# Six edits to the instruction order of a one-core hybrid encoder layer: two loads, one scaling pass, one transpose pair, three splits, four merges and five casts

## The chip, the cores and the metric

The kernel runs on one core of a Trainium2 chip. The metric is the device time of one execution in microseconds (us), as the median of several runs. The engines are named as in the profile: PE (TensorE, matmuls), DVE (VectorE), ACT (ScalarE), POOL (GpSimd) and SP (SyncE, whose queue issues nearly all DMAs here).

## The reference

One layer of a bidirectional hybrid encoder, for 1024 tokens of width 1024:

```python
x = layer_norm(x, emb_ln_g, emb_ln_b)
proj = x @ w_in                                  # 1024 -> 5120
q, k, v, z_a, u, z_b, g_a, g_b = split(proj)     # 4x512, 2x512, 2x1024
attn = neighbourhood_attention(q, k, v, rpb)     # 8 heads x 64, window 8 x 16 on a 16 x 64 grid
y_a  = attn * silu(z_a)
u    = centred_depthwise_conv(u, conv_w, conv_b)
h    = rg_lru(u, ..., forward) + rg_lru(u, ..., reverse)   # gates, then a linear scan over the tokens
y_b  = h * silu(z_b)
m    = sigmoid(g_a + b_merge[0]) * (y_a @ w_ba) + sigmoid(g_b + b_merge[1]) * (y_b @ w_bb)
out  = layer_norm(ALPHA * x + m @ w_out, ln_g, ln_b)
```

## The kernel before

All is in fp32 accuracy: each operand of a product is split into a high and a low part (a rounding copy, called a cast, and a subtraction, called a low split), and each product is three matmuls (`mm3`, line 139): high x high, high x low, low x high. The instruction order of every engine is the order in which the program records it; no scheduler moves anything. So a line that is written earlier stands earlier in its engine's queue, and every engine, SP too, works through its queue in order.

The stages, with their place in the profiled span:

- Prologue (to about 80 us): LayerNorm statistics of the token tiles, turning them, and the products for v, q and k. Tiles 4 to 7 are loaded already turned; their mean and scale are brought into rows by two transposes of a broadcast column (`spread(i)`, line 322, into the bank bcp) and a copy (`spread_copy`, line 326). The scale `ln6e` comes from a chain of small DVE operations that ends in line 245.
- The remaining columns of `x @ w_in`, in 17 pairs of 7 products (a Strassen-like scheme, so that a 2 x 2 block product takes 7 products): 119 slots plus 4, each 12 matmuls of 512 columns on PE. `pair` p uses weights `wa_*`, `ws_*` (tags a11, s2, s3, s1, a12, s4, a22) that are loaded, summed on DVE (`s_sum`), cast on ACT or POOL (`s_hi`, line 476) and split on DVE or POOL (`s_lo`, line 133). `evacuate` takes finished products off their banks: the copies `u` on ACT, the sums `c` and `s` on DVE (lines 775, 811). `c` frees the bank that the next pair of products writes.
- Beside the slots, at slots that tables name, run other steps (`todo`): the conv, gates and scans of the RG-LRU (lines 842 to 937; POOL's pass in line 918 stands behind a memset on DVE in line 917), and the token passes: `tokens_in` loads tile hw4 to hw7, `tokens_scaled` is ACT's pass over 128x1024 (line 1046), `tokens_gained` POOL's four (line 1050), `tokens_out` the store. `TOKENS_AT` holds, for each tile, the slots of the load, the scaling and the four gains.
- Slots 116 and on load q, k and the bias of the first heads (`load_k`, `load_head`: qs, ks, bias). At the end of the pairs (`ending(k)`) the first two products of the lru branch are made into the banks mb100 and mb101; `b_gate` (line 1137) multiplies them with the merge gate `g` on DVE: m <- g, mb. `g` was stored to DRAM (gb_d) as slots made it and is loaded by `g_load` (line 1124).
- Attention, 8 heads of 8 units. A unit has the scores on PE (line 1214), softmax on DVE and ACT, transposes of the probabilities (line 1236) and the values (`acc`, line 1262), in two value banks. `finish_a` (line 1273) reads a finished value bank into `attn` on DVE. Between them PE gets the remaining products of the lru branch as a filler; their `b_gate` waits in the list `pending` for the next unit's place for it, as `finish_a` and its followers wait in `todo`.
- Then the products of the attention branch, the merge, w_out, and the last LayerNorm (from about 530 us).

The lines that the change touches in the loop over slots and in the loop over units are these:

```python
        for o in lows:          # slots: the low split of the slot before
            s_lo(*o)
        lows = [prep]
...
        for f in pending:       # units: b_gate, and the split of the next weights
            f()
        pending.clear()
        for f in todo.pop(unit, ()):   # finish_a, finish_v, gated
            f()
```

Of the kernel before, what the change touches and what calls it, by code (L numbers as in the profile page):

```python
# [33 lines left out]
GATE_AT = (21, 31, 42, 52, 63, 73, 84, 94)  # L34
LATE_AT = (109, 109, 110, 111, 112)
HEAD_AT = 116
TOKENS_AT = ((1, 3, (4, 4, 5, 5)), (2, 5, (6, 6, 7, 7)), (3, 7, (8, 8, 9, 9)), (9, 11, (12, 12, 13, 13)))
RATES_AT = 14
LO_POOL = ("a11", "a22")
HI_POOL = ("a12", "s2", "s1", "s3", "s4")  # L40
FIRST_POOL = ("a22", "s4")
FIRST_ACT = (1, 2, 3)
U_PAIRS = (1, 6)
BLOCKS = (1, 0, 6, 4, 3, 2, 5, 7)
SCORES = (0, 1, 2, 5, 6, 7, 3, 4)
# [26 lines left out]
def encoder_kernel(ctx, tc, x, xt, gb1, gb, w_qk, w_v, w_s, w_ba, w_bb, w_gate, smalls, bias, w_out, out):  # L72
# [245 lines left out]
    def spread(i):  # L318

        bcp[i] = pst.tile([P, HALF], F32, tag="bank", name=f"bcp{i}")  # L320
        for z, col in enumerate((sts[i][1][:, 0:1], sts[i][2])):
            PE.transpose(bcp[i][:, z * P:(z + 1) * P], col.to_broadcast([P, P]), ident[:])
# [12 lines left out]
    def affine(i, *kks):  # L335
        for kk in kks or BOTH:
            tps[i, kk] = pst.tile([P, HALF], F32, tag="bank", name=f"tp{i}_{kk}")
            for k4 in range(4):
                k = 4 * kk + k4
                g, b = (sm[:, SM_LN + 8 * z + k:SM_LN + 8 * z + k + 1] for z in range(2))  # L340
                A.activation(tps[i, kk][:, k4 * P:(k4 + 1) * P], xts[i][:, k, :], AF.Identity, bias=b, scale=g)
            turn_hi(i, kk)
            if kk == 0:
                tag = ("a22", "a21", "a12", "a22")[i - 4]
                tt[i, 3] = wsp.tile([P, 4, P], F32, tag=tag, bufs=2 if tag == "a22" else 1, name=f"t3_{i}")[:]
                A.copy(tt[i, 3], tp4(i, 0))
# [30 lines left out]
    def f(t, i):  # L377
        return t[:, :, ti(i)].bitcast(F32)
# [27 lines left out]
    def v_part(i, kind, ks):  # L406

        if i not in vos:
            vos[i], vn[i] = bank(f"v{i}"), 0
        for k in ks:  # L410
            a = blocks[k // 4][i // 4][kind == "a"][:, k % 4, ti(i)]
            PE.matmul(vos[i][:], a, wv[kind == "w"][k][:], start=vn[i] == 0, stop=vn[i] == 23)  # L412
            vn[i] += 1
# [37 lines left out]
    s_a, s_w = {}, {}  # L451
# [21 lines left out]
    def s_hi(p, o):  # L473
        if p < N_PAIR:
            s_w[p, o] = pair(wsp, [P, 4, P], f"w{o}_{p}", tag="w" + o)
            (G.tensor_copy if p and o in HI_POOL and p not in FIRST_ACT else A.copy)(s_w[p, o][0][:], s_a[p, o])

    def s_lo(p, o):
        if p < N_PAIR:
            hi, lo = s_w[p, o]  # L480
            lo_of(G if o in (LO_POOL if p else FIRST_POOL) else V, lo[:], s_a[p, o], hi[:])
# [149 lines left out]
    v_hi(2)  # L631
    v_part(3, "w", K1)
    v_part(3, "a", K0)
    spread(6)
    spread_copy(6)
    affine(4, 0)
    ln_sums(7)
    centred(6)
    v_lo(2)
    v_store(2)  # L640
    affine(4, 1)
    sts_rest(7)
    v_part(3, "a", K1)
    v_hi(3)
    lows_t(4)
    v_lo(3)
# [178 lines left out]
    todo = {}  # L825

    def at(slot, pos, f):
        todo.setdefault((slot, pos), []).append(f)
# [147 lines left out]
    def yb_lo(t):  # L976
        hi, lo = late["yb"]
        lo_of(V, lo[:, t, :], lo[:, t, :].bitcast(F32), hi[:, t, :])
# [92 lines left out]
    for t, slot in enumerate(LATE_AT[1:]):  # L1071
        at(slot, 1, lambda t=t: yb_load(t))
        at(slot + 2, 1, lambda t=t: yb_hi(t))
        at(slot + 3, 0, lambda t=t: yb_lo(t))
    at(HEAD_AT, 1, head_pool)
    at(HEAD_AT, 1, lambda: load_k(0))
    at(HEAD_AT, 1, lambda: load_head(1))
# [43 lines left out]
    def g_load(which, j, n, **kw):  # L1121
        if j < NK:
            g = mt[which, j, n] = ev.tile([P, HALF], F32, name=f"g{which}{j}{n}", **(kw or dict(tag="z", bufs=5)))
            SP.dma_start(g[:], (ga_d, gb_d)[which][j][:, n * HALF:(n + 1) * HALF])
# [16 lines left out]
    def ending(k):  # L1141

        if k == 0:
            for pl in (hts.pop(), hts.pop(), wsp, hb):
                pl.release()
            late["mp"] = pool("mp")
        if k == 2:
            b_load(1, 2)
            for n in range(2):
                g_load(1, 1, n)  # L1150
        if k < 2:
            g_load(1, 0, k)
            late["o", k] = bank(f"mb10{k}")
            run(b_group(1, 0, k, late["yb"], late["o", k]))
        if 0 < k < 3:
            b_gate(1, 0, k - 1, late["o", k - 1])
# [3 lines left out]
    for slot in range(7 * N_PAIR + 4):  # L1160
        p, k = divmod(slot, 7)
        if k == 0 and p < N_PAIR:
            takers[p], ub[p] = takes[p](), {}
        done = (p, k - 1) if k else (p - 1, 6)
        prep = (p + 1, OPS[k - 1]) if k else (p if p else N_PAIR, OPS[6])
        rest = evacuate(*done) if slot <= 7 * N_PAIR else []
        s_hi(*prep)
        for f in todo.pop((slot, 0), ()):
            f()
        for f in squashes:  # L1170
            f()
        squashes = rest[:1]
        stores[slot + 2] = rest[1:]
        if p < N_PAIR:
            product(p, k)
        for o in lows:
            s_lo(*o)
        lows = [prep]
        for f in stores.pop(slot, ()):
            f()  # L1180
        if k < 4:
            s_sum(p + 1, ("s1", "s2", "s3", "s4")[k])
        elif k == 4:
            s_load(p + 2, "a11", "a21", "a12", "a22")
        for f in todo.pop((slot, 1), ()):
            f()
        if p == N_PAIR:
            ending(k)
# [38 lines left out]
    def exped(h, t):  # L1227
        w = P * len(near(t))
        A.activation(probs[h % 2][t][:], scs.pop((h, t))[:, :w], AF.Exp, bias=sums[h][0][:, t:t + 1], scale=-1.0,  # L1229
                     accum_out=sums[h][1][:, t:t + 1])  # L1230
# [112 lines left out]
    for unit in range(-NT, H * NT + PV_LAG):  # L1343
        h, c = divmod(unit, NT)
        before, b = divmod(unit - 1, NT)
        pv, pb = divmod(unit - PV_LAG, NT)

        if -1 <= before < H - 1:
            biased(before + 1, SCORES[b])
        if 0 <= before < H:  # L1350
            turned_lo(before, BLOCKS[b])
        if 0 <= h < H:
            turned(h, BLOCKS[c])
            if c == 3:
                sums_turned(h, tps[h, BLOCKS[c]])
        if 0 <= pv < H:
            values(pv, BLOCKS[pb])
            if pb in (5, 7) and pv < H - 1:
                for d, f in enumerate((finish_a, finish_v) + ((gated,) if pv % 2 else ())):
                    todo.setdefault(unit + d + 1, []).append(lambda f=f, pv=pv, g=pb // 7: f(pv, g))  # L1360
            elif pb in (5, 7):
                for d, f in enumerate(last_half(pb // 7)):
                    todo.setdefault(unit + d + 1, []).append(f)
        if 0 <= h < H:
            turned_hi(h, BLOCKS[c])
            if c == 2:
                sums_inverted(h)
            elif c == 3:
                sums_out(h)
        if -1 <= before < H - 1:  # L1370
            exped(before + 1, SCORES[b])
        for f in pending:
            f()
        pending.clear()
        for f in todo.pop(unit, ()):
            f()
        if -1 <= h < H - 1:
            score(h + 1, SCORES[c])
        if 0 <= h < H:
            if c == (4 if h == H - 1 else 5 if h % 2 else 7):  # L1380
                sums_in(h)
            elif c == (6 if h == H - 1 else 7) and h % 2:
                for n in range(2):
                    gate(h // 2, n)
        if c == 0 and 0 <= h:
            load_head(h + 2)
            if h % 2:
                load_za(h // 2)
        if c == PV_LAG and 0 <= h and h % 2 == 0:
            load_v(h // 2 + 1)  # L1390
        want = sum(FILL[:h + 1]) + FILL[min(h + 1, H)] * (c + 1) // NT
        while filled < want and next(fill, True) is None:
            filled += 1
        if unit == H * NT:

            for pl in (late["hd"], late["hd0"], late["ybp"]):
                pl.release()
            wop = pool("wop", "right")
            raw = {}

            def w_load(o, c):
                k, n = ("b11", "b12", "b21", "b22").index(o) // 2 * 4 + c, int(o[2]) - 1
                t = raw[o, c] = wop.tile([P, HALF], F32, tag=f"{o}{c}", name=f"w{o}_{c}")
                SP.dma_start(t[:], w_out[k * P:(k + 1) * P, halves[n]])

            b_load(0, 1)
            for n in range(2):
                g_load(0, 0, n, **(dict(tag="u3", bufs=1) if n else {}))
            for c in range(2):
                w_load("b12", c)  # L1410
                w_load("b11", c)
# [468 lines left out]
```

## Time and profile before

| what | value |
|---|---|
| runs | 660.69 us median of 3 (659.84 to 660.7) |
| profiled execution | 660.51 us; its span 658.6 us |
| granted PE clock | 0.997 |
| busy, share of the span | PE 98%, DVE 81%, ACT 62%, POOL 62% |
| DMA | 118.66 MB, mean 180 GB/s |

The span runs from the first to the last instruction on the core; the execution's time has 1.9 us more. Busy time of a pipelined engine counts overlapping instructions once. In rows of the timeline, the first number is the start in us of the span, the second the duration, and a bracket says how long the engine was idle before and what ended it. Numbers such as L1137 are lines of the kernel before.

### The profile page before, as it was taken

The numbers are of one execution on the slowest core, as the hardware profiler recorded it, in microseconds if no ns is written. First come the engines' busy times: TensorE is split into PE (matmuls) and PEld (weight loads), VectorE is DVE, ScalarE is ACT, GpSimd is POOL, SyncE is SP. The second block draws the span as 40 slices with busy tenths as digits, with TensorE's granted clock in tenths as the row PEclk, the third lists the DMA queues.
The fourth block names the chain that finished last, engine by engine and source line by source line (L and its number), as shares of the span: only waits on it lengthen the run. The fifth ranks groups of instructions, "written<-read, shape, count | busy, mean of one in ns | idle before, by whom it ended". The sixth has DMA issues, their size and how long they took to land.

```text
span 658.6 us, 9484 instructions
## 1 busy us (share of the span) xinstructions
PE 646.0 (98%) x3089; PEld 539.3 (82%) x3089; DVE 536.8 (81%) x850; ACT 409.4 (62%) x731; POOL 409.5 (62%) x331
## 2 busy tenths in 40 slices
PE   8999999999999999999999999999999999999994
PEld 6888878888888887888788888789888888888884
DVE  7989998995998699879988696277887876994777
ACT  5578655467786676778566834277777744574243
POOL 6569669824676476567656555012652549989956
PEclk9999999999999999999999999999999999999998
DMA  8765577333344124531461547897976288333023
GB/s 325 289 220 162 190 245 260 119 127 112 127 144 135 42 98 124 180 117 59 159 209 61 196 159 269 309 341 261 365 278 239 65 305 295 117 116 127 17 111 128
DMA packets 54064, 118.66 MB, mean 180 GB/s; under 512 B 5680, under 2 KB 10368, under 8 KB 52480
## 3 DMA queue, kind: packets, MB, share of 16 engines
q1 hardware_dynamic: 53696, 117.67, 51.5%
q8 instruction: 24, 0.39, 0.2%
q10 hardware_dynamic: 320, 0.40, 0.2%
q14 instruction: 24, 0.20, 0.1%
HBM read 82.36 MB, written 35.68 MB: 179 GB/s over the span
## 4 chain that ended last, share of the span: by engine, by line
PE 89%; DVE 8%; DMA 2%; issue 1%; ACT 0%; SPq 0%; DVEq 0%; ACTq 0%
PE a L139 32%; PE mb L139 12%; PE s L139 12%; PE v L412 6%; PE x L139 5%; PE w L139 5%; PE acc L1262 4%; PE q L139 3%; PE s L1214 3%; PE pt L1236 3%; PE g L884 2%; DMA g<-gb_d 1%; DVE ws_l L133 1%; DVE uc L842 1%; PE tp L358 1%
## 5 line engine op out<-in xcount | busy, mean ns | idle before, releaser
L139 PE MATMUL a<-ht_h,ws_h 128*128 128x512 f32 x136 | 53.1, 390 | 0.0
L139 PE MATMUL a<-ht_l,ws_h 128*128 128x512 f32 x136 | 52.9, 389 | 0.0
L139 PE MATMUL a<-ht_h,ws_l 128*128 128x512 f32 x136 | 52.9, 389 | 0.0
L139 PE MATMUL a<-b_h,wa_h 128*128 128x512 f32 x136 | 52.9, 389 | 0.0
L139 PE MATMUL a<-b_h,wa_l 128*128 128x512 f32 x136 | 52.9, 389 | 0.0
L139 PE MATMUL a<-b_l,wa_h 128*128 128x512 f32 x136 | 52.9, 389 | 0.0
L1224 DVE CUSTOM_DVE_ANT_0 sc<-s,bias 128x384 f32<-128x384 f32 (+1 forms) x64 | 33.4, 523 | 20.3 <-PE s L1214 11.4
L1243 ACT CAST pt_h<-pt 128x384 fp32r<-128x384 f32 x64 | 29.0, 454 | 23.8 <-PE pt L1236 19.3
L1229 ACT ACTIVATE p<-sc,summ 128x384 f32<-128x384 f32 (+1 forms) x64 | 37.8, 591 | 6.2 <-DVE summ L1224 5.9
L139 PE MATMUL mb<-ya,wb_h 128*128 128x512 f32 x128 | 39.5, 389 | 0.0
L992 POOL CAST wb_h<-wb 128x512 fp32r<-128x512 f32 x9 | 7.0, 780 | 49.5 <-DMA wb<-in_w_bb_dram 49.5
L133 DVE TENSOR_TENSOR pt_l<-pt,pt_h 128x384 fp32r<-128x384 f32 x64 | 33.2, 519 | 1.9 <-ACT pt_h L1243 1.6
L412 PE MATMUL v<-wv,b_h 128*128 128x512 f32 x128 | 32.7, 397 | 0.3 <-ACT b_h L513 0.3
L1214 PE MATMUL s<-ks,qs 128*128 128x384 f32 (+1 forms) x128 | 31.9, 330 | 0.4 <-DVE m L1137 0.4
L1638 POOL TENSOR_TENSOR z<-z,gb 128x512 f32<-128x512 f32 (+1 forms) x22 | 25.9, 1190 | 9.0 <-ACT z L1633 8.2
L139 PEld LDWEIGHTS a<-ht_h,ws_h 128*128 128x128 f32 x136 | 25.5, 188 | 5.8 <-issue 0.5
L1236 PEld LDWEIGHTS pt<-ident,p 128*128 128x128 f32 x176 | 23.2, 140 | 8.3
L139 PEld LDWEIGHTS a<-ht_l,ws_h 128*128 128x128 f32 x136 | 25.5, 188 | 5.4
L139 PEld LDWEIGHTS a<-b_h,wa_h 128*128 128x128 f32 x136 | 25.5, 188 | 5.3
L139 PEld LDWEIGHTS a<-b_l,wa_h 128*128 128x128 f32 x136 | 25.5, 188 | 5.3
L139 PEld LDWEIGHTS a<-b_h,wa_l 128*128 128x128 f32 x136 | 25.5, 188 | 5.3
L139 PEld LDWEIGHTS a<-ht_h,ws_l 128*128 128x128 f32 x136 | 25.5, 188 | 5.2
(578 smaller groups left out, 2300.8 us busy)
## 6 DMA issues: line engine op xcount, KB each, us to landing
ks<-k_d SPq DMA_DIRECT2D x8, 1024.0 KB, 8.3
v_d<-vs SPq DMA_DIRECT2D x8, 512.0 KB, 3.1
q_d<-q SPq DMA_DIRECT2D x8, 512.0 KB, 3.0
ga_d<-ga SPq DMA_DIRECT2D x16, 256.0 KB, 2.0
gb_d<-gb SPq DMA_DIRECT2D x16, 256.0 KB, 2.3
k_d<-k SPq DMA_DIRECT2D x8, 512.0 KB, 3.6
qs<-q_d SPq DMA_DIRECT2D x8, 512.0 KB, 5.9
g<-gb_d SPq DMA_DIRECT2D x16, 256.0 KB, 5.9
```

The lines of the kernel that those rows point to most:

```text
L133: eng.tensor_tensor(lo, full, hi.bitcast(F32), ALU.subtract)
L139: PE.matmul(o, a, b, start=first and i == 0, stop=last and i == len(prods) - 1, skip_group_check=not (first and last))
L412: PE.matmul(vos[i][:], a, wv[kind == "w"][k][:], start=vn[i] == 0, stop=vn[i] == 23)
L884: PE.matmul(o[:, n, :], w[:, 2 * d + b, :], us[b][:, n * HALF:(n + 1) * HALF], start=z == 0, stop=z == 1)
L992: G.tensor_copy(hi[:], st[:])
L1214: PE.matmul(o[:, :P * len(near(t))], q[:, t * P:(t + 1) * P], k[:, z, keys], start=z == 0, stop=z == 1)
L1224: V.tensor_tensor_reduce(s[:, :w], o[:, :w], heads[h][2][:, b0:b0 + w], -1.0, 3.0e38, ALU.add, ALU.min, accum_out=sums[h][0][:, t:t + 1])
L1229: A.activation(probs[h % 2][t][:], scs.pop((h, t))[:, :w], AF.Exp, bias=sums[h][0][:, t:t + 1], scale=-1.0, accum_out=sums[h][1][:, t:t + 1])
L1236: PE.transpose(tp[:, n * P:(n + 1) * P], probs[h % 2][t][:, z * P:(z + 1) * P], ident[:])
L1243: A.copy(pt[0][:, span(b)], tps[h, b][:, :P * len(near(b))])
L1262: PE.matmul(acc[n][:, lo - n * HALF:hi - n * HALF], vvs[h // 2][:, b, h % 2, :], pt[:, a:a + hi - lo], start=b in (1, 6) and z == 0, stop= ...
L1638: G.tensor_tensor(z, z, gbs[c, n][:, part], (ALU.mult, ALU.add)[c])
```

## The change

In the kernel after, all lines from the first table on stand one line further down, later ones up to five.

```diff
-TOKENS_AT = ((1, 3, (4, 4, 5, 5)), (2, 5, (6, 6, 7, 7)), (3, 7, (8, 8, 9, 9)), (9, 11, (12, 12, 13, 13)))
+TOKENS_AT = ((1, 4, (4, 4, 5, 5)), (2, 5, (6, 6, 7, 7)), (3, 7, (8, 8, 9, 9)), (9, 11, (12, 12, 13, 13)))
...
-FIRST_ACT = (1, 2, 3)
+HI_ACT = (1, 2, 3, 16)
+HELD = (32, 60, 81)
...
-            (G.tensor_copy if p and o in HI_POOL and p not in FIRST_ACT else A.copy)(s_w[p, o][0][:], s_a[p, o])
+            (G.tensor_copy if p and o in HI_POOL and p not in HI_ACT else A.copy)(s_w[p, o][0][:], s_a[p, o])
...
     v_part(3, "a", K0)
+    affine(4, 0)
+    v_part(3, "a", K1)
     spread(6)
     spread_copy(6)
-    affine(4, 0)
     ln_sums(7)
...
     affine(4, 1)
     sts_rest(7)
-    v_part(3, "a", K1)
     v_hi(3)
...
+    for n in BOTH:
+        at(HEAD_AT - 1, 1, lambda n=n: g_load(1, 0, n))
     at(HEAD_AT, 1, head_pool)
...
         if k < 2:
-            g_load(1, 0, k)
             late["o", k] = bank(f"mb10{k}")
...
-        for o in lows:
-            s_lo(*o)
-        lows = [prep]
+        if slot in HELD:
+            lows.append(prep)
+        else:
+            for o in lows:
+                s_lo(*o)
+            lows = [prep]
...
+        for f in todo.pop(unit, ()):
+            f()
         for f in pending:
             f()
         pending.clear()
-        for f in todo.pop(unit, ()):
-            f()
```

The scaling of tile hw4 goes from slot 3 to slot 4. In pair 16, the casts of a12, s2, s1, s3 and s4 go from POOL to ACT. In slots 32, 60 and 81 (the fifth products of pairs 4, 8 and 11) the waiting low split is held for one slot and done with the next one. In the prologue, the last four `v` matmuls of tile 3 and half of the affine step of tile 4 come ahead of the transposes of tile 6. The loads of g for mb100 and mb101 go from slots 119 and 120 to slot 115. In the attention's units, the value bank's step stands ahead of `b_gate`, where both fall into one unit (four times).

On SP, around the heads' first loads (gb_d is the store of a merge gate, g its load), the queue before reads:

```order
L785 DMA gb_d<-gb_3924 128x512
L785 DMA gb_d<-gb_3975 128x512
L1014 DMA ks_4032<-k_d 128x1x2048
L1008 DMA qs_4034<-q_d 128x1024
L1009 DMA bias_4035<-in_bias_dram 128x896
L1014 DMA ks_4038<-k_d 128x1x2048
L785 DMA gb_d<-gb_4042 128x512
L1124 DMA g_4080<-gb_d 128x512
L785 DMA gb_d<-gb_4056 128x512
L1124 DMA g_4097<-gb_d 128x512
```
and after:

```order
L786 DMA gb_d<-gb_3924 128x512
L1127 DMA g_4008<-gb_d 128x512
L1127 DMA g_4010<-gb_d 128x512
L786 DMA gb_d<-gb_3975 128x512
L1015 DMA ks_4036<-k_d 128x1x2048
L1009 DMA qs_4038<-q_d 128x1024
L1010 DMA bias_4039<-in_bias_dram 128x896
L1015 DMA ks_4042<-k_d 128x1x2048
L786 DMA gb_d<-gb_4046 128x512
L786 DMA gb_d<-gb_4060 128x512
```
The two loads of g stood between the stores of gb at the end of this piece; now they stand right behind its first store, ahead of another store and of the loads of ks, qs, bias and ks.

On DVE, in slots 80 to 82, before (k belongs to the branch's own splits, c and s are the sums that free the product banks):

```order
L907 SCALAR_TENSOR_TENSOR w_1_3092<-r_1_2954,w_1_3092 128x1024
L133 TENSOR_TENSOR ws_12_l<-s_12f,ws_12_h 128x512
L133 TENSOR_TENSOR k_3095<-a_11_3073,k_3095 128x512
L811 TENSOR_TENSOR c_11_3172<-u_11_3143,a_11_3049 128x512
L917 MEMSET w_1_3092 128x1
L133 TENSOR_TENSOR ws_12_l<-s_12f,ws_12_h 128x512
L811 TENSOR_TENSOR s_11_3126<-u_11_3119,s_11_3126 128x512
```
and after:

```order
L908 SCALAR_TENSOR_TENSOR w_1_3092<-r_1_2954,w_1_3092 128x1024
L134 TENSOR_TENSOR k_3095<-a_11_3073,k_3095 128x512
L812 TENSOR_TENSOR c_11_3171<-u_11_3143,a_11_3049 128x512
L918 MEMSET w_1_3092 128x1
L134 TENSOR_TENSOR ws_12_l<-s_12f,ws_12_h 128x512 x2
L812 TENSOR_TENSOR s_11_3126<-u_11_3119,s_11_3126 128x512
```
The first of the splits `ws_12_l` stands behind `c` and the memset now, beside the next one.

On ACT, in slots 2 to 5 (`u` takes a product off its bank, CAST are the casts of pair 1, `hw` the scaling passes), before:

```order
L476 CAST ws_1_h<-s_1f 128x512
L798 ACTIVATE q_1132<-a_0_1110 128x512
L1046 ACTIVATE hw_1125<-hw_1125,kept 128x1024
L1101 COPY u_0_1178<-s_0_1159 128x512
L476 CAST ws_1_h<-s_1f 128x512 x2
L1046 ACTIVATE hw_1151<-hw_1151,kept 128x1024
```
and after:

```order
L477 CAST ws_1_h<-s_1f 128x512
L799 ACTIVATE q_1132<-a_0_1110 128x512
L1104 COPY u_0_1177<-s_0_1159 128x512
L477 CAST ws_1_h<-s_1f 128x512
L1047 ACTIVATE hw_1125<-hw_1125,kept 128x1024
L477 CAST ws_1_h<-s_1f 128x512
L1047 ACTIVATE hw_1151<-hw_1151,kept 128x1024
```
The first scaling pass stands behind `u` and a cast, one slot ahead of the second pass.

## The prediction

> **What bounds the kernel now.** I read the page first (span, busy shares, the chain that ended last), then the list of what TensorE waits for, then the timeline of TensorE row by row at each of those waits.
>
> ```profile
> span 658.6 us, 9484 instructions
> PE 646.0 (98%) x3089; PEld 539.3 (82%) x3089; DVE 536.8 (81%) x850; ACT 409.4 (62%) x731; POOL 409.5 (62%) x331
> PE 89%; DVE 8%; DMA 2%; issue 1%; ACT 0%; SPq 0%; DVEq 0%; ACTq 0%
> ```
>
> The profiled execution took 660.51 us, so 1.9 us lie around its span of 658.6; the median of the three runs is 0.18 us higher. TensorE (PE) is busy for 646.0 us and does the same 3089 matmuls after the change. So no engine's work matters for itself: what can be had is part of the 12.6 us in which PE is not busy, and whatever moves on another engine counts only through a wait of PE. The list of PE's waits (total us, count, longest) names four that lie where the diff works:
>
> ```profile
> PE s L1214 <- DVE m L1137: 0.4, 1, 0.4
> PE bcp L322 <- DVE ln6e L245: 0.4, 1, 0.4
> PE a L139 <- DVE w L917: 0.4, 1, 0.4
> PE s L139 <- ACT u L1101: 0.2, 1, 0.2
> ```
>
> Each happens once, which suits a change that moves single instructions. The list is too small, though: matmuls are pipelined and a row's duration runs on into the next one's, so a stall is better read from the distance between starts. Undisturbed, that distance is this (columns of the timeline: start us, duration us, engine, line, operation):
>
> ```profile
> 317.53 0.39 PE L139 MATMUL s<-b_h,ws_l 128*128 128x512 f32 x1
> 317.75 0.39 PE L139 MATMUL s<-b_l,ws_h 128*128 128x512 f32 x1
> ...
> 517.26 0.49 PE L1236 MATMUL pt<-ident,p 128*128 128x128 f32 x3
> 517.50 0.31 PE L1262 MATMUL acc<-pt_h,vv 128*128 128x128 f32 x1
> ```
>
> A 512-column matmul takes 0.23 us to the next start, three 128-column transposes together 0.24, so one about 0.08. Every stall below is a distance less these.
>
> **The change, part by part.**
>
> Spread of tile 6. In the prologue, the two transposes into bcp now come behind four more `v` matmuls.
>
> ```profile
> 36.93 0.27 PE L322 MATMUL bcp<-ident,ln6m 128*128 128x128 f32 x1
> 37.58 0.32 PE L322 MATMUL bcp<-ident,ln6e 128*128 128x128 f32 x1 [0.38 <-DVE ln6e L245]
> ...
> 37.31 0.21 DVE L245 TENSOR_SCALAR ln6e<-ln6e 128x1 f32<-128x1 f32 x1
> ```
>
> The second transpose starts 0.65 us after the first, for VectorE's (DVE) last step of the statistics ends at 37.52. Four matmuls first are 4 x 0.23 = 0.9 us, which puts the transposes at 37.8, after 37.52. The gain is 0.65 - 0.1 = 0.55 us (bounds: the 0.38 that the wait is given, and 0.57). The copy of bcp on ScalarE (ACT) and what uses it come some 0.4 us later; ACT works next to this on the casts of tile 4, which come earlier by as much, so I put their cost at nothing. If that cover is thinner, up to the 0.55 is lost, not more, since PE then stands as it stood.
>
> Tokens. ACT's scaling pass over 128x1024 (tile hw, line 1046) leaves slot 3 for slot 4.
>
> ```profile
> 93.25 0.39 PE L139 MATMUL a<-ht_l,ws_h 128*128 128x512 f32 x1
> 93.86 0.50 PE L139 MATMUL s<-b_h,ws_h 128*128 128x512 f32 x1 [0.22 <-ACT u L1101]
> ...
> 92.10 1.24 ACT L1046 ACTIVATE hw<-hw,kept 128x1024 f32<-128x1024 f32 x1
> 93.23 0.57 ACT L1101 COPY u<-s 128x512 f32<-128x512 f32 x1
> ```
>
> PE goes from 93.25 to 93.86, 0.61 for 0.23: it stands 0.38 us until the copy `u`, queued behind the scaling pass, gives its bank free. Without the pass `u` starts about 1.1 us earlier and ends near 92.7, ahead of the 93.48 at which PE wants it: 0.38 gained. What is late next: the pass itself, and GpSimd's (POOL) gains and offsets on the same tile, about a slot less than the gap (near 1.1 us). POOL is full there until about 122 us, so all its work of that stretch comes 1.1 us later; the first of it that PE needs are low splits, ready 6 us or more before their matmuls by the dependences I followed. Cost nothing; if that room were not there, at most the 1.1 us once.
>
> Held splits. In three slots the low split of the prep before (ws_l, on DVE) stands behind the sums that free PE's bank.
>
> ```profile
> 318.52 0.50 PE L139 MATMUL a<-ht_h,wa_h 128*128 128x512 f32 x1 [0.38 <-DVE w L917]
> ...
> 316.17 1.09 DVE L133 TENSOR_TENSOR ws_l<-s_12f,ws_h 128x512 fp32r<-128x512 f32 x1
> 317.79 0.68 DVE L811 TENSOR_TENSOR c<-u,a 128x512 f32<-128x512 f32 x1
> ...
> 256.59 0.39 PE L139 MATMUL s<-b_l,ws_h 128*128 128x512 f32 x1
> 256.95 0.50 PE L139 MATMUL a<-ht_h,wa_h 128*128 128x512 f32 x1
> ```
>
> In slot 81 PE goes from 317.75 (above) to 318.52, 0.77 for 0.23: a stall of 0.54, and it starts right after `c` (317.79 + 0.68 = 318.47), although the row names the short memset that ends last. The split ahead of it occupies DVE from 316.17 until `k` at 317.19, 1.0 us; taken out, `c` ends at 317.45 and PE does not wait: 0.54. In slot 60 the distance is 0.36, a stall of 0.13, with the same order on DVE. Slot 32 I take as slot 60 but for the next sum there, which is as tight: 0.1. Together 0.77 (bounds 0.5, if only slot 81 follows, and 0.8). The split itself is needed some slots later; and DVE has idle time behind all three.
>
> Does the split cost more where it now stands? Behind the memset POOL begins its pass over w:
>
> ```profile
> 318.67 2.65 POOL L918 TENSOR_TENSOR w<-i,w 128x1024 f32<-128x1024 f32 x1 [1.95 <-DVE w L917]
> 319.59 2.28 DVE L133 TENSOR_TENSOR ws_l<-s_12f,ws_h 128x512 fp32r<-128x512 f32 x1
> ```
>
> A split beside that pass takes 2.28 us, alone 0.68 to 1.09. Before, one split of this slot meets the pass; after, the second of the held pair meets it, and the later one no longer does. So the number of long splits stays at one, and only the sum between them (line 811) comes some 1.2 us later; the matmul that follows it has about 3 us of room. I cost it at nothing (bounds: 0 and 0.67, the whole gain of slots 60 and 81). [...]
>
> Loads of g. The two loads of 256 KB for the first merge gates leave SyncE's queue (SP) behind the heads' loads for a place ahead of them.
>
> ```profile
> 425.42 0.39 PE L139 MATMUL mb<-yb_l,wb_h 128*128 128x512 f32 x1
> 426.23 0.50 PE L1214 MATMUL s<-ks,qs 128*128 128x256 f32 x2 [0.42 <-DVE m L1137]
> ...
> 425.48 0.69 DVE L1137 SCALAR_TENSOR_TENSOR m<-g,mb 128x512 f32<-128x512 f32 x1 [7.10 <-DMA g<-gb_d]
> ...
> 417.25 8.14 DMA g<-gb_d
> ...
> 405.34 5.71 SPq L785 DMA_DIRECT2D gb_d<-gb  x2
> 412.24 0.55 SPq L1014 DMA_DIRECT2D ks<-k_d  x1
> ...
> ks<-k_d SPq DMA_DIRECT2D x8, 1024.0 KB, 8.3
> ```
>
> The first scores matmul takes the bank that `m` reads. `m` waits 7.1 us for `g`, which was issued at 417.25 and took 8.14 us beside the megabytes of ks; PE goes from 425.42 to 426.23, 0.81 for 0.23: 0.58 lost. After, the issue stands behind the store of 405.34, with the DMA engines nearly idle from 409 to 411 us; even 8.14 us from 406 end at 414, and `m` then follows its product near 423. The second `m` follows likewise, before PE wants its bank at 427.3. Gain 0.58 (bounds 0.42 and 0.6). Moved past on SP: one store of gb, ks, qs, bias, ks and a store, each later by two issues of some 0.6 us at the worst. ks at 412.24 plus 8.3 us lands near 420.5, used at 425.6: 5 us of room.
>
> Value banks. At four places DVE does `attn` (line 1273, frees the value bank) ahead of `m`, each 0.6 to 0.7 us.
>
> ```profile
> 461.58 0.27 PE L1281 MATMUL pt<-ident,sums 128*8 128x128 f32 x1
> 461.82 0.44 PE L1262 MATMUL acc<-pt_h,vv 128*128 128x384 f32 x1
> ...
> 477.26 0.49 PE L1236 MATMUL pt<-ident,p 128*128 128x128 f32 x3
> 477.76 0.45 PE L1262 MATMUL acc<-pt_h,vv 128*128 128x384 f32 x1
> ...
> 499.71 0.27 PE L1281 MATMUL pt<-ident,sums 128*8 128x128 f32 x1
> 499.83 0.45 PE L1262 MATMUL acc<-pt_h,vv 128*128 128x384 f32 x1
> ...
> 515.25 0.49 PE L1236 MATMUL pt<-ident,p 128*128 128x128 f32 x3
> 515.88 0.44 PE L1262 MATMUL acc<-pt_h,vv 128*128 128x384 f32 x1
> ```
>
> Against 0.24 for three transposes the second pair (0.50) lost 0.26 and the fourth (0.63) 0.39; against 0.08 for the short one the first (0.24) lost 0.16 and the third (0.12) 0.04. `attn` 0.6 us earlier covers each. Of the fourth I count 0.3, as PE's next bank is nearly as late. Sum 0.76 (bounds 0.3, if the next waits take most of it back, and 0.85). `m` comes 0.7 us later, and its bank has a unit of room (some 4 us).
>
> Casts of pair 16. Five casts of 128x512 move from POOL to ACT. Neither engine is over 62% busy and PE shows no wait there: 0 (bounds: 0.3 either way, half of a 128x512 copy on ACT, 0.57 in the row of `u`; a gain where DVE's splits meet less of POOL, a loss where a cast stands ahead of a copy).
>
> Sum: 0.55 + 0.38 + 0.77 + 0.58 + 0.76 = 3.04 us, from 660.51 to 657.5. With all lower bounds (0.38 + 0 + 0.5 + 0.42 + 0.3 = 1.6) it is 658.9, with all upper ones (0.57 + 0.38 + 0.8 + 0.6 + 0.85 + 0.3 = 3.5) 657.0.
>
> **The rivals.**
>
> Part of it is taken back. The gains are small against the room of the next waits: PE may only pull ahead as far as DVE and ACT do, and DVE works without a pause through slots 0 to 4 and before slot 81. For it: the second bank in such a slot is free only 0.1 to 0.5 us before its use. Against it: those operations wait for PE's own products, so they come earlier with it. Losing the spread's 0.55 and half of the held and the attention terms (0.77) gives 3.04 - 1.3 = 1.7: 658.8.
>
> All of it comes back elsewhere: the early lead runs into a term that does not follow PE, such as DVE's work, 81% of the span, bound by itself from 286 to 318 us. For it, the chain's 8% on DVE. Against it, 0.58 + 0.76 lie behind that stretch, where DVE has room. Then 660.0, within 0.2%.
>
> [...]
>
> The other side: SP's queue works in order, and the two loads of g need free buffers and stored gates. If they stand there, the heads' ks stand behind. ks costs nothing until it is issued later than 425.6 - 8.3 = 417.3, and from then PE loses a us for each; to eat the remaining 2.5 us and 1.3 more it must slip to 421.1, 9 us. The stores that g needs were issued at 397 to 403 and stores of gb land in about 2.5 us, which speaks against. Then 662.
>
> **How the numbers follow.** 0.2% (1.3 us) is about what a measurement of this kernel can tell from no change. Forecast (656.6 to 658.0) 0.58; part taken back (658.0 to 659.3) 0.20; the exclusion 0.04; all taken back 0.13; queue held 0.05. The first three are faster by over 0.2% (under 659.4): 0.82; same 0.13; slower 0.05. The range leaves out the last two and a little below: 656.4 to 659.4.
>
> **What the profile would show.** Right: the four waits of the second fence are gone, `m` no longer waits for g, the chain has no DMA of g, and the four distances before acc are near 0.24 and 0.1; POOL has five casts less, ACT five more; PE's busy time stays at 646 and the span shrinks to about 655.5. Wrong: a new row among PE's waits on DVE's `c` or `s` in the slots behind 32, 60 and 81, on ACT's `u` in slots 4 and 5, or on DMA ks near 425.

## The result and the profile after

The changed kernel takes 658.91 us (median of 12 runs, 658.8 to 659.29), the kernel before 660.69 us (12 runs, 659.84 to 660.81). The medians differ by 1.78 us (0.27%), the two profiled executions (660.51 and 658.89 us) by 1.62; the ratio of the two kernels on record is 0.9977, 95% interval 0.9968 to 0.9985. So the kernel became faster, by between half and six tenths of the 3.04 us that were forecast. Below, "after" is the changed kernel, and its line numbers stand one to five further on than those of before.

First the page of after, then its list of what PE waits for (total us, count, longest):

```profile
span 657.1 us, 9484 instructions
...
PE 76%; DVE 13%; issue 3%; POOL 3%; DMA 2%; ACT 2%; SPq 0%; DVEq 0%; POOLq 0%; ACTq 0%
```

```profile
PE a L140 <- DVE w L918: 1.1, 1, 1.1
...
PE a L140 <- DVE c L776: 0.3, 1, 0.3
```

The span is 1.5 us shorter. The four waits that the prediction named are gone, and two new ones stand on the list, both on DVE. The first of them has the name of an old one (`a` for `w`, now line 918), but it lies at 196.6 us, where the old one lay at 318.5. The chain has 3% of POOL, of which there was none, and DVE has gone from 8% to 13%.

The starts of the same matmul in the two traces, subtracted, tell where each part of the time went. The next table gives by how much PE's lead over the kernel before grew (minus) or shrank (plus) in each stretch, worked out from the starts at its two ends; `no32` is an experiment told below.

| stretch of before, us | what lies there | forecast | after | no32 |
|---|---|---|---|---|
| 0 to 36 | start | 0 | +0.01 | -0.13 |
| 36 to 40 | spread of tile 6 | -0.55 | -0.60 | -0.60 |
| 80 to 95 | scaling pass out of slot 3 | -0.38 | -0.51 | -0.51 |
| 130 to 140 | slot 19's sum (new) | 0 | +0.59 | +0.56 |
| 175 to 180 | behind held slot 32 | -0.1 | -0.29 | 0.00 |
| 180 to 198 | slot 39's sum (new) | 0 | +1.68 | -0.05 |
| 250 to 260 | behind held slot 60 | -0.13 | -0.32 | -0.30 |
| 310 to 320 | behind held slot 81 | -0.54 | -0.69 | -0.64 |
| 424 to 428 | loads of g | -0.58 | -0.70 | -0.69 |
| 428 to 519 | value banks | -0.76 | -0.66 | -0.67 |

The stretches between move by 0.05 us at most. The columns sum to -3.04, -1.51 and -3.04 with those. Each of the gains came, 3.8 us in all; two losses, 0.59 and 1.68 us, took 2.3 us of them back.

How the removed stalls look now, in the timeline of after, at the places shown of before:

```profile
92.65 0.39 PE L140 MATMUL a<-ht_l,ws_h 128*128 128x512 f32 x1
92.88 0.39 PE L140 MATMUL s<-b_h,ws_h 128*128 128x512 f32 x1
...
318.29 0.39 PE L140 MATMUL s<-b_l,ws_h 128*128 128x512 f32 x1
318.52 0.39 PE L140 MATMUL a<-ht_h,wa_h 128*128 128x512 f32 x1
318.75 0.39 PE L140 MATMUL a<-ht_h,wa_l 128*128 128x512 f32 x1
...
425.28 0.39 PE L140 MATMUL mb<-yb_l,wb_h 128*128 128x512 f32 x1
425.51 0.40 PE L1219 MATMUL s<-ks,qs 128*128 128x256 f32 x2
...
513.90 0.49 PE L1241 MATMUL pt<-ident,p 128*128 128x128 f32 x3
514.14 0.42 PE L1267 MATMUL acc<-pt_h,vv 128*128 128x384 f32 x1
```

Every distance is the undisturbed 0.23 or 0.24. And the two new stalls:

```profile
133.45 0.39 PE L140 MATMUL s<-b_l,ws_h 128*128 128x512 f32 x1
134.10 0.50 PE L140 MATMUL a<-ht_h,wa_h 128*128 128x512 f32 x1 [0.26 <-DVE c L776]
...
195.10 0.39 PE L140 MATMUL s<-b_l,ws_h 128*128 128x512 f32 x1
196.60 0.50 PE L140 MATMUL a<-ht_h,wa_h 128*128 128x512 f32 x1 [1.12 <-DVE w L918]
```

0.65 and 1.50 us from start to start where 0.23 would do: 0.42 and 1.27 lost, with 0.1 each that the matmul behind a stall takes longer to the next start. Both are the same step of a pair: DVE's sum `c`, which frees the product bank, comes too late. (The row for the second names the short memset of `w`, which ends last, at 196.61; `c` starts at 195.87, takes 0.68 and ends at 196.55.) The other 0.31 of the 1.68 is a small stall at 189.80 us, 0.46 from the start before, where PE waits for ACT's copy `u` (189.09 us, 0.57 long).

**The large one.** Slot 39's sum is seven slots behind the held split of slot 32. These are DVE's and POOL's operations in between, first before and then after (`uc` is a tap, one step of the conv; `gw_l` is the low split of gate weights; `i<-i,uc` is the product of the gate i and uc):

```profile
177.10 1.27 DVE L842 SCALAR_TENSOR_TENSOR uc<-up,sm,uc 128x1024 f32<-128x1024 f32 x1
...
180.00 1.27 DVE L842 SCALAR_TENSOR_TENSOR uc<-up,sm,uc 128x1024 f32<-128x1024 f32 x1
181.19 2.88 DVE L133 TENSOR_TENSOR ws_l<-s_5f,ws_h 128x512 fp32r<-128x512 f32 x1
184.00 1.78 DVE L471 TENSOR_TENSOR s_6f<-a_6f 128x512 f32<-128x512 f32 x1
...
195.01 0.68 DVE L775 TENSOR_TENSOR c<-u,a 128x512 f32<-128x512 f32 x1
...
177.17 2.35 POOL L133 TENSOR_TENSOR gw_l<-gw,gw_h 128x512 fp32r<-128x512 f32 x1 [0.67 <-ACT gw_h L857]
180.23 3.30 POOL L894 TENSOR_TENSOR i<-i,uc 128x1024 f32<-128x1024 f32 x1 [0.70 <-ACT i L891]
```

```profile
175.29 1.70 DVE L134 TENSOR_TENSOR ws_l<-s_5f,ws_h 128x512 fp32r<-128x512 f32 x2
176.91 2.31 DVE L843 SCALAR_TENSOR_TENSOR uc<-up,sm,uc 128x1024 f32<-128x1024 f32 x1
...
179.74 2.90 DVE L134 TENSOR_TENSOR ws_l<-s_5f,ws_h 128x512 fp32r<-128x512 f32 x1
182.56 2.32 DVE L843 SCALAR_TENSOR_TENSOR uc<-up,sm,uc 128x1024 f32<-128x1024 f32 x1
...
185.82 1.79 DVE L472 TENSOR_TENSOR s_6f<-a_6f 128x512 f32<-128x512 f32 x1
...
176.64 1.50 POOL L134 TENSOR_TENSOR gw_l<-gw,gw_h 128x512 fp32r<-128x512 f32 x1 [0.20 <-ACT gw_h L858]
179.70 2.39 POOL L895 TENSOR_TENSOR i<-i,uc 128x1024 f32<-128x1024 f32 x1 [1.56 <-ACT i L892]
182.05 1.75 POOL L134 TENSOR_TENSOR wa_l<-a_5f,wa_h 128x512 fp32r<-128x512 f32 x1
```

Look at the starts. Before, DVE's tap (uc) starts at 177.10, POOL's split at 177.17: the tap takes 1.27 and POOL's operation is the long one, 2.35. The next tap at 180.00 is again ahead of POOL's product at 180.23, which takes 3.30; only the split at 181.19 comes second, and takes 2.88. After, the held pair of splits stands ahead of the tap, POOL starts first at 176.64, 179.70 and 182.05, the first two of its operations are short (1.50, 2.39), and DVE's are the long ones (2.31, 2.90, 2.32). On these two operations POOL gained 1.8 us. DVE needs 8.91 us from the first of these taps to the sum s_6f, where it needed 6.90, and reaches it at 185.82 instead of 184.00, although PE's lead before slot 32 was 0.5 us. Before, slot 39's `c` ended at 195.69 and PE took its bank at 195.83, without a stall: there were 0.14 us of room.

**The small one.** At 121.5 us after, DVE's sum takes 1.79 us, beside POOL's passes over hw, which are still running; before, it came behind their end and took 0.69. So DVE starts its tap at 123.2 in both kernels, and PE's whole lead of 1.1 us is cut back to 0.5 where the sum of slot 19 is due:

```profile
112.67 9.79 POOL L1050 TENSOR_TENSOR hw<-hw,ln_row 128x512 f32<-128x512 f32 x6
...
122.60 0.69 DVE L471 TENSOR_TENSOR s_3f<-s_3f,a_3f 128x512 f32<-128x512 f32 x1
123.21 1.28 DVE L842 SCALAR_TENSOR_TENSOR uc<-up,sm,uc 128x1024 f32<-128x1024 f32 x1
```

```profile
113.14 9.60 POOL L1051 TENSOR_TENSOR hw<-hw,ln_row 128x512 f32<-128x512 f32 x6
...
121.50 1.79 DVE L472 TENSOR_TENSOR s_3f<-s_3f,a_3f 128x512 f32<-128x512 f32 x1
123.22 1.27 DVE L843 SCALAR_TENSOR_TENSOR uc<-up,sm,uc 128x1024 f32<-128x1024 f32 x1
```

### The profile page after: what moved, and what is told of

The parts are those of the page before. It is cut to its first block, busy times and chain, and to the rows that moved or that the text cites. A ratio compares the mean times of both kernels' runs of the same rounds, so it can differ in the third digit from the quotient of the medians.

```text
span 657.1 us, 9484 instructions
## 1 busy us (share of the span) xinstructions
PE 644.3 (98%) x3089; PEld 539.3 (82%) x3089; DVE 536.1 (82%) x850; ACT 412.2 (63%) x736; POOL 400.5 (61%) x326
## 4 chain that ended last, share of the span: by engine, by line
PE 76%; DVE 13%; issue 3%; POOL 3%; DMA 2%; ACT 2%; SPq 0%; DVEq 0%; POOLq 0%; ACTq 0%
PE a L140 27%; PE mb L140 13%; PE s L140 10%; PE x L140 5%; PE w L140 5%; PE acc L1267 3%; PE s L1219 3%; PE pt L1241 3%; PE v L413 2%; POOL hw L1051 2%; PE g L885 2%; DVE uc L843 1%; DVE ws_l L134 1%; DMA ln_row<-in_gb_dram 1%; ACT tp L342 1%
```

## The experiments

Theory A: the held split of slot 32 lets POOL start ahead of DVE, and DVE pays. Theory B: DVE just can't follow PE's lead. For slot 19, theory C: the moved scaling pass brings POOL's full stretch later against PE, and DVE is held up beside it; theory D: the lead alone does it. Each kernel was timed beside the kernel before; the place-by-place readings come from one trace of each.

**no32**: `HELD = (60, 81)` in the kernel after.

> The kernel after with only slots 60 and 81 held. Theory A (the split held at slot 32 makes DVE start the following taps and splits just behind POOL's operations instead of just ahead of them, and DVE is late by 1 us or more when slot 39's sum is due): the new stalls of PE near 190 us (0.24) and 196 us (1.28) are gone, the old stall of slot 32 (0.13) is back, so 658.9 - 1.4 = about 657.5 us. Theory B (the lead that PE gained earlier is what DVE cannot follow; the held split has little to do with it): a stall of 0.4 us or more stays at 196 us, 658.3 us or more.

657.64 us (657.38 to 657.78), ratio 0.9952 (0.9939 to 0.9964). The last column of the table above is this kernel: the stretch 180 to 198 costs nothing, slot 32's gain is gone, and the rest is as after but for 0.13 us at the start. PE's lead here is no smaller than that of after (0.69 us at 175 against 0.54), so theory B fell. The tap starts at 176.40, ahead of POOL's split at 176.48, and takes 1.27 as before.

**only32**: `HELD = (32,)` and nothing else of the change, on the kernel before.

> The kernel before with nothing but the low split of slot 32 held. Theory A: PE gains 0.13 us behind slot 32 and loses about 0.9 us (1.28 less the lead that the kernel after had there) before slot 40, so 661.3 to 661.8 us, slower than before. Theory B: no change, 660.5 us.

662.23 us, ratio 1.0022 (1.0013 to 1.0031): this edit alone makes the kernel slower. In its trace PE loses 1.64 us between 180 and 198 and gains 0.28 ahead of it; DVE's taps take 2.31 and 2.32 and its split 2.90, as in after, without any lead. The time lies above the 661.3 to 661.8 that were expected: the loss is not smaller for want of a lead.

**clear32**: the kernel after; POOL's two operations come later.

```diff
-        at(slot + 3, 1, weights_lo)
+        at(slot + (6 if t == 1 else 3), 1, weights_lo)
...
-        at(slot + 4, 0, gated_input)
+        at(slot + (6 if slot == 31 else 4), 0, gated_input)
```

> The kernel after, slot 32 still held, but POOL's two large operations that DVE meets there (the low split of the second gate weights, and the product of i and uc in the gate stage that begins at slot 31) come three and two slots later. Theory A: the tap near 177 us takes about 1.3 us instead of 2.31 and the split near 180 us about 1 us instead of 2.90, and the stall near 196 us (1.28) is gone or under 0.3: about 657.6 us. Theory B: the stall stays at 1 us, 658.9 us. If POOL's later work meets other DVE operations instead, the stall is in between.

660.17 us, ratio 0.9991 (0.9982 to 1.0): slower than after. At the place itself theory A held: the tap took 1.27 and the split 0.68. But POOL's product came at 185.09 and its split at 189.69, and each met one of DVE's next two splits instead:

```profile
177.01 1.27 DVE L843 SCALAR_TENSOR_TENSOR uc<-up,sm,uc 128x1024 f32<-128x1024 f32 x1
...
178.80 0.68 DVE L134 TENSOR_TENSOR ws_l<-s_5f,ws_h 128x512 fp32r<-128x512 f32 x1
...
185.90 2.67 DVE L134 TENSOR_TENSOR us<-uc,us 64x1024 fp32r<-64x1024 f32 x1 [0.71 <-ACT us L849]
...
190.31 2.21 DVE L134 TENSOR_TENSOR us<-uc,us 64x1024 fp32r<-64x1024 f32 x1
...
197.36 0.50 PE L140 MATMUL a<-ht_h,wa_h 128*128 128x512 f32 x1 [1.97 <-DVE w L918]
```

Those splits took 1.22 each in after. Moving POOL's work moved the collision, and the stall grew to 2.1 us. The run settled the local step and not the whole. (The last section has what else this kernel lost.)

**delay32**: the kernel after, with three passes over 128x8 on POOL ahead of its split.

```diff
             hi, lo = ucs[t][2]
+            for _ in range(3 if t == 1 else 0):
+                G.tensor_scalar(t2[:], t2[:], 1.0, None, ALU.mult)
             lo_of(G, lo[:], ucs[t][3][:], hi[:])
```

> The kernel after, slot 32 held, with three idle passes over 128x8 (about 0.9 us in all, on a scratch tile nobody reads) on POOL ahead of its low split of the second gate weights: work is added, none is taken away. Theory A (order of arrival between POOL and DVE): the tap near 177 us now starts ahead of POOL and takes 1.3 us instead of 2.31, the next split ends before POOL's product of i and uc, and PE's stall near 196 us (1.28) is gone: about 657.5 us. Theory E (it is the amount of work that POOL and DVE have there, or the held split's own length): the stall stays or grows, 658.9 us or more.

658.89 us, ratio 0.9974 (0.9964 to 0.9984): no change against after, which theory A did not expect. The tap did win (176.98, 1.27 us), but the three passes took 2.17 us beside the held splits, POOL's split ran until 179.9 and its product came right behind it, ahead of the next tap:

```profile
176.49 2.17 POOL L863 TENSOR_SCALAR sp<-sp 128x8 f32<-128x8 f32 x3
...
179.87 2.85 POOL L897 TENSOR_TENSOR i<-i,uc 128x1024 f32<-128x1024 f32 x1
180.39 3.41 DVE L843 SCALAR_TENSOR_TENSOR uc<-up,sm,uc 128x1024 f32<-128x1024 f32 x1
```

There is one collision less and one more. So this run, the one in which only the order was to change, does not tell theory A from theory E.

**omit32**: the kernel after, slot 32 held, POOL's split three slots later and its product left out, so that this kernel computes something else.

```diff
+        if slot != 31:
             at(slot + 4, 0, gated_input)
```

> The kernel after, slot 32 still held, but POOL's product of i and uc in the gate stage that begins at slot 31 is left out (that stage's scan then takes i alone), and the low split of the second gate weights comes three slots later. Theory A (the held split costs because DVE and POOL take turns on their operations, and POOL's 2.4 to 3.3 us there fall on DVE): DVE's splits and taps from 177 to 182 us take 0.7 to 1.3 us each, slot 39's sum ends before PE wants it, and PE's stall near 196 us is gone: about 657.5 us. Theory F (the held split delays DVE by its own order, with or without POOL): the stall stays at 1 us or more, 658.9 us.

657.35 us, ratio 0.9961 (0.9948 to 0.9973). DVE has the same instructions as after, in the same order, and the stall is gone:

```profile
176.83 1.27 DVE L843 SCALAR_TENSOR_TENSOR uc<-up,sm,uc 128x1024 f32<-128x1024 f32 x1
...
179.23 1.27 DVE L843 SCALAR_TENSOR_TENSOR uc<-up,sm,uc 128x1024 f32<-128x1024 f32 x1
...
194.24 0.68 DVE L776 TENSOR_TENSOR c<-u,a 128x512 f32<-128x512 f32 x1
...
194.85 0.39 PE L140 MATMUL s<-b_l,ws_h 128*128 128x512 f32 x1
195.08 0.40 PE L140 MATMUL a<-ht_h,wa_h 128*128 128x512 f32 x1
```

From 180 to 198 us PE loses 0.11 us here and not 1.68. So the held split costs next to nothing by its own place in DVE's order; it costs through POOL's work behind it, as only32 says from the other side. That the order of arrival went with which of the two engines paid is read from the rows: before and no32 on one side, after and only32 on the other, have the same operations there, and the winners change with the held split, with a lead or without (the tap takes 1.27 us in the first two, 2.31 in the others; POOL's split 2.35 and 1.50). No run changed that order and nothing else.

**no32_tok3**: no32 with `TOKENS_AT[0]` back at `(1, 3, ...)`.

> As no32, and the scaling pass of tile hw4 back in slot 3. Theory C (the later scaling pass moves POOL's full stretch 93 to 123 us later against PE, and DVE, which shares that stretch with it, comes late to slot 19's sum): PE's stall near 93 us (0.38) is back and that near 134 us (0.43) is gone, so the time is that of no32 within 0.2 us. Theory D (the stall near 134 us comes from the lead of the spread alone): it stays at 0.4 us and the time is 0.4 us above no32.

657.4 us, ratio 0.9949 (0.9937 to 0.9961). PE's stall at 93 us is back (+0.51 against no32), that at 134 us is gone (-0.54), and the last matmul starts 0.03 us from no32's. In this state of the kernel the moved scaling pass is worth nothing: theory C.

**no32_free**: no32 with the last gain pass at slot 17, `(9, 11, (12, 12, 13, 17))`.

> As no32, and the last of POOL's sixteen gain passes (tile hw7) moved from slot 13 to slot 17, behind POOL's full stretch. Theory C (POOL's full stretch, which ends at 122.7 us, holds DVE's second sum of pair 3 and so slot 19's sum): POOL ends about 1.6 us earlier there, DVE's sum near 121.5 us takes 0.7 us instead of 1.79, and PE's stall near 134 us (0.43) is gone: 657.2 us. Theory D (nothing of POOL holds that sum): the stall stays, 657.6 us.

657.42 us, ratio 0.9955 (0.9942 to 0.9967). Half of it came: the sum near 122 us takes 0.69. But the moved pass pushed POOL's next split to 129.60, where a later sum of DVE met it (130.11, 1.77 us for 0.68), and a loss of 0.6 stayed. (The profiled run took 658.31 us, the other four 657.37 to 657.52; it had lost 0.6 at 47 us already.) It is settled that this sum's duration goes with POOL's stretch (0.69 us here, 1.79 in after), and not how to be rid of the stall.

**no32_p16**: no32 with `HI_ACT = (1, 2, 3)`.

> As no32, and the five casts of pair 16 back on POOL. By the prediction these casts are worth nothing: 657.6 us, and no step of over 0.1 us between the two kernels' matmuls from 370 to 410 us. Rival: DVE's splits of pair 16 meet more of POOL and PE waits 0.3 us or more.

658.04 us, ratio 0.9961 (0.9949 to 0.9974). Against before, PE's lead stays at 1.16 to 1.17 us from 320 to 424 us: the five casts are worth nothing, as forecast. (The median is 0.4 above no32; in the profile 0.5 us of lead is missing by 20 us already, long before pair 16.)

**no32_nog**: no32 with the loads of g back in slots 119 and 120.

> As no32, and the loads of g for the first two merge gates back in slots 119 and 120. By the prediction PE's stall of 0.58 us near 425 us is back and nothing else changes: 658.2 us. Rival (the DMA engines' backlog at 412 to 425 us, not the loads' place, sets when g lands, so that the loads' place changes little): 657.6 us.

658.08 us, ratio 0.9963 (0.995 to 0.9977): 0.44 over no32. The two profiled runs differ by 0.95, of which 0.5 lies ahead of 20 us. The stall did not come back as told: `m` waited for g again, but PE lost only 0.05 us at the first scores matmul, and 0.2 more by 426.4 us.

```profile
423.69 0.69 DVE L1138 SCALAR_TENSOR_TENSOR m<-g,mb 128x512 f32<-128x512 f32 x1 [6.57 <-DMA g<-gb_d]
...
424.16 0.39 PE L140 MATMUL mb<-yb_l,wb_h 128*128 128x512 f32 x1
424.43 0.51 PE L1218 MATMUL s<-ks,qs 128*128 128x256 f32 x2
```

From g's issue (415.94) to `m` it took 7.75 us here, 8.2 before. So the late loads stand at the edge: in the trace of before PE lost 0.58 and 0.2 by it, here 0.05 and 0.2. Why the wait was shorter here was not tried. (The rest of the 0.95 lies at 465 and 490 us; 0.14 at 465 is also in no32_p16, whose loads are early.)

**nohold**: no32 with `HELD = ()`.

> As no32, with slots 60 and 81 not held either. By the prediction PE's stalls of 0.13 and 0.54 us behind them are back and nothing else: 0.67 above no32, 658.3 us. [...]

658.51 us, ratio 0.9971 (0.996 to 0.9981). In its trace the stretches 250 to 260 and 310 to 320 gain 0.02 and 0.00 against before, where no32 gains 0.30 and 0.64: the two held splits are worth 0.9 us, where 0.67 was expected.

**noattn**: no32 with `pending` ahead of `todo` again.

> As no32, with b_gate ahead of the value bank's step again. By the prediction the four stalls ahead of acc are back: 0.76 above no32, 658.4 us. Rival (the next waits in the same units take most of it back): 0.3 above, 657.9 us.

658.22 us, ratio 0.9967 (0.9955 to 0.998). From 428 to 519 us it gains 0.00 against before, no32 0.67: that is the term.

**no32_again**: no32 once more.

> The kernel no32 once more, to see how far the median of one kernel moves between two sets of runs: 657.6 us, within 0.3.

658.28 us (657.52 to 658.43), ratio 0.9966 (0.9953 to 0.9978): 0.64 above the first time, and not within the 0.3 expected. Its profile has 0.55 less lead at 20 us (a wait for a weight tile at 12 us) and 0.2 less each at 47 and 85. So two medians here can differ by 0.6 us without a cause in the code, and the terms above rest on the traces, not on such differences. It also means that no32's gain over after (1.27 or 0.63 us by the medians, 1.4 at the place) is sure in the place, and less so in its size.

## Why the prediction was wrong

The forecast of 657.5 is what the change gives without slot 32; with it, half of the gain is lost. That no32 comes to just the same 3.04 us is in part luck: it loses 0.56 at slot 19, which the forecast put at nothing, and gains about as much by stalls that were counted too short and by 0.13 at the start. The prediction's own sign of being wrong, a new wait on DVE behind a held slot, is there: it is the one of 1.1 us. By its own steps:

- Spread: 0.60 for 0.55. Right; what follows on ACT was hidden, as PE's lead does not change from 40 to 80 us.
- Tokens: 0.51 for 0.38 at the place, but 0.59 was lost at slot 19. The step that failed is "cost nothing": it followed POOL's own results to PE (no wait of PE on POOL is on the list of after), and not DVE, whose sum beside POOL's stretch got longer (1.79 us, 0.69 before). The 1.1 us once that stood as its bound holds the 0.59, but the sum of lower bounds left it out.
- Held splits: this is the step that decided. "Slot 32 I take as slot 60" and "DVE has idle time behind all three" were wrong for slot 32. The busy times of the stretches behind the three slots, which could have been read of before, say so (PE, PEld, DVE, ACT, POOL, clock):

```profile
172.00:196.00 24.00, 24.00 (x106) 19.48 (x105) 23.86 (x23) 18.35 (x22) 15.67 (x11) 1.00 0.35 116
256.00:280.00 24.00, 24.00 (x107) 19.54 (x106) 21.81 (x27) 15.68 (x20) 15.56 (x10) 1.00 0.61 198
318.00:342.00 24.00, 23.62 (x104) 19.44 (x104) 21.85 (x26) 15.24 (x20) 15.60 (x10) 1.00 0.71 241
```

DVE has 2.2 us free of 24 behind slots 60 and 81, and 0.14 behind slot 32. There the lengthened DVE operations reach slot 39's sum, which had 0.14 us of room. The term was sized at -0.1 and measured -0.29 + 1.68 = +1.39.

- The exclusion, with its chance of 0.04, is a term that no run shows; what the runs showed in its place are longer operations where DVE and POOL work at the same time. At slots 60 and 81 it went as the working said: the second split of the held pair meets POOL's pass over w (2.89 us from 318.51, beside a pass from 318.18), the sum behind it comes late (321.32), and PE does not notice. At slot 32 the operations behind the held pair, two taps of 128x1024 and a split (2.31, 2.32 and 2.90 us, before 1.27, 1.27 and 1.19), meet three POOL operations, and the working did not go through this.
- Loads of g: 0.70 for 0.58 at the place, and 0.09 more in a step at 428.12, which the table has in its last row. But with the loads late, in no32_nog, PE lost 0.26 and not 0.79, so what the move is worth depends on how long g then takes.
- Value banks: 0.66 for 0.76 (0.57 without that step); the next wait took some of the fourth back, as allowed for: in after, PE goes from 515.27 to 515.72 there, 0.45 for 0.23.
- Pair 16: 0, as forecast.
- A size that was off everywhere: behind a stall the first matmul takes 0.1 us more to the next start (318.52 to 318.86 before, to 318.75 after; 0.33 us before behind the stalls at 93.86 and 256.95), so each stall of 512-column matmuls was counted 0.1 short.
- The premise that what can be had is part of the 12.6 us in which PE is not busy was off. After, PE is busy for 644.3 us and not busy for 12.8, so the 1.5 us came out of the busy time. A matmul's row lasts 0.39 us and the next starts after 0.23, so the first 0.16 us of each stall counts as busy.

Together: 1.49 for slot 32 and 0.46 for the tokens (0.59 lost, less the 0.13 more gained at the place) make 1.95; the other terms gave 0.4 more than forecast; 3.04 - 1.95 + 0.4 is the 1.5 that came.

## What to carry to other kernels

Before a move is costed at nothing, read how busy the engine is behind that very place: three places with the same edit differed in 0.14 or 2.2 us of free time, and only at the full one did the edit cost more than it gained. Where DVE and POOL work at the same time, a reordering on one engine can change who starts first; in the pairs shown, the operation that started second took longer (a tap 2.31 us for 1.27, POOL's product 3.30 for 2.39). So look at starts close together (in those pairs 0.04 to 0.96 us apart) and price both outcomes for all operations until the next idle time, not for the moved one alone. Of a bundle of small edits, compare the same matmul's start in both traces; it shows each gain and each loss where medians differ by less than they scatter.

## What the runs showed of the hardware

In the pairs shown, order of arrival went with who paid between DVE and POOL: before, DVE's tap started first by as little as 0.07 us (177.10 against 177.17) and took 1.27 us, and POOL's split took 2.35; after, POOL's split started first (176.64) and took 1.50, and the tap took 2.31.

In clear32 PE waited 1.97 us, and about 1.3 us after it went on, the granted clock fell to half for some 3 us (0.50 in each us from 199 to 202), which it did not behind the 1.12 us of after (1.00 in each stretch from 190 to 204; busy time of PE, PEld, DVE, ACT and POOL in stretches of 2 us, then the clock):

```profile
196.00:198.00 2.00, 0.64 (x3) 0.55 (x4) 2.00 (x6) 1.85 (x2) 0.49 (x1) 1.00 0.99 307
198.00:200.00 2.00, 2.00 (x8) 1.58 (x7) 2.00 (x2) 1.27 (x3) 2.00 (x1) 0.67 0.46 164
200.00:202.00 2.00, 2.00 (x7) 1.52 (x6) 2.00 (x2) 0.18 (x1) 1.17 (x2) 0.50 0.35 131
```

In that time a matmul took 0.43 us to the next start (199.83 to 200.26), and PE lost 1.6 us more than by the wait itself: this is most of why the profiled run of clear32, 661.27 us, is slower than after. The fall of the clock seems to come in some executions of that kernel only: of its eleven times five lie at 659.45 to 659.69 us, four, the profiled one among them, at 661.12 to 661.58, about as much higher as PE lost by the clock, and two at 660.17 and 660.27. No other of them has a trace.
